# A fifth Strassen pair in the gates of two branches, and every second low part of the projections added up by transfers

## The chip, the cores and the metric

The kernel runs on one core of a Trainium2 chip. The metric is the device time of one execution in microseconds. TensorE (PE) multiplies, VectorE (DVE) and ScalarE (ACT) work element by element, GpSimd (POOL) does a little of that here and issues some transfers, and SyncE's queue (SP) issues the loads of the weights. Each engine works through its own instructions in order and waits for others by semaphores.

## The reference

One layer of a decoder trunk: one input projection feeds three mixers, each mixer's output is projected to the model width, the three results are merged by sigmoid gates computed from the input, and an output projection, a residual and a layer norm follow. All is float32, with 256 rows of 2048 channels.

```
u = x @ w_in[l]
(a_q, a_f, a_i, a_g, b_q, b_k, b_v, b_g,
 c_b, c_c, c_x, c_g, m_a, m_b, m_c) = jnp.split(u, split_idx, axis=-1)
o_a = hgrn2_mixer(a_q, a_f, a_i, lower_bounds[l])
o_a = o_a * lax.rsqrt(jnp.mean(jnp.square(o_a), axis=-1, keepdims=True) + RMS_EPS)
o_a = o_a.reshape(bsz, t, HGRN_WIDTH) * hgrn_norm_g[l].astype(jnp.float32)
y_a = (o_a.astype(x.dtype) * jax.nn.silu(a_g)) @ w_proj_hgrn[l]
o_b = swa_sink_attention(b_q, b_k, b_v, bias, attn_sinks[l])
y_b = (o_b * jax.nn.silu(b_g)) @ w_proj_attn[l]
o_c = short_gated_conv(c_b, c_c, c_x, conv_w[l])
y_c = (o_c * jax.nn.silu(c_g)) @ w_proj_conv[l]
merged = jax.nn.sigmoid(m_a) * y_a + jax.nn.sigmoid(m_b) * y_b + jax.nn.sigmoid(m_c) * y_c
y = merged @ w_out[l]
x = layer_norm(ALPHA * x + y, ln_g[l], ln_b[l])
```

## The kernel before

Every product of float32 operands is made of three matmuls. An operand is split into a high part `hi` (ScalarE casts it to fp32r, L114) and a low part `lo` (VectorE subtracts the high part from the raw value, L115), and TensorE adds hi x hi, hi x lo and lo x hi. x and the mixers' outputs are split once and stay in SBUF. The weights stream through: SP loads 1 MB granules `raw` (three buffers), each in two halves of 1024 columns (in the projections two k-tiles of 512), and each half is split into `hi` and `lo` (four buffers each) and used 12 times by TensorE. A program's scheduler sets the order of the instructions of each engine ahead of time.

The program has three parts. Up to about 525 us it does the input projections and the mixers; a list of generators, `tasks`, is advanced one step by `pump` behind every half granule, so that the mixers' work lies between the matmuls. From about 526 to 900 us it does the three branches, each in two halves: the gate's weights (`pair_of_groups`, 16 k-tiles as eight pairs p = 0..7, two output groups of 512 columns at once), and then two projections (`gemm`, four granules for each half in all), whose results are multiplied with the gates and added into `merged`. Then come the output projection (its first two groups by `pair_of_groups` too), residual and layer norm.

In `pair_of_groups` the pairs 1, 3, 5 and 7 go by Strassen's scheme (Winograd's form): the 2 x 2 blocks (two k-tiles by two column groups) of weights are added and subtracted into four sums, in a tile `w` of their own (L702 to L704), these are split into `hw` (ScalarE) and `lw` (VectorE), and seven products of blocks do instead of eight. A product is three matmuls of 512 columns (L677 to L679). The matching sums of x are made once, by `sums_of_x`, ahead of the branches, and those of the merged rows by `turn`. Eight partial sums p1 to p8 stay in PSUM until the last pair; then `one` is a copy of p1 and eight additions on VectorE (L727 to L734) give the two groups.

Of the kernel before, what the change touches and what calls it, by code (L numbers as in the profile page):

```python
# [44 lines left out]
PAIRS = (0, 1, 0, 1, 0, 1, 0, 1)  # L45
# [5 lines left out]
def hybrid_kernel(ctx, tc, a, out):  # L51
# [6 lines left out]
    lop = ctx.enter_context(tc.tile_pool(name="lop", bufs=4))  # L58
# [96 lines left out]
    def gemm(src, xs, n, major, first=None):  # L155
# [6 lines left out]
        for g in range(src.shape[0]):  # L162
# [4 lines left out]
            for s in range(2):  # L167
                hi, lo = halves[s] if first else split_w(raw[:, s])
# [31 lines left out]
    def constants():  # L200
# [15 lines left out]
        c["gn"] = const.tile([P, HW], F32, name="gn")  # L216
        nc.sync.dma_start(out=c["gn"], in_=a["hgrn_norm_g"].partition_broadcast(P))
# [335 lines left out]
    def sums_of_x():  # L553

        n = len(pairs)
        xr = rawp.tile([P, n, 2, T], F32, tag="raw", name="xr")
        for i, p in enumerate(pairs):
            nc.sync.dma_start(out=xr[:, i], in_=a["xT"][:, 2 * p : 2 * p + 2])
# [3 lines left out]
        for i in range(0, n, 2):  # L562
            dst = t8([P, 2, 4, 2, P], "sums", F32R)
            sums.append(dst)
            for j in range(2):
                split_to(dst[:, j], sx[:, :, i + j])
            yield
# [81 lines left out]
    msums = []  # L649

    def turn(m, d):
        dst = t8([P, 4, 2, T], "m", F32R)
        ms.append(dst)
        if d % 2 == 0:
            msums.append(t8([P, 2, 4, 2, P], "msums", F32R))
        for i, ps in transpose_pairs([[m[:, t, c * P : c * P + P] for t in range(2)] for c in range(4)], "mT"):
            split_to(dst[:, i : i + 2], ps)
            if PAIRS[2 * d + i // 2]:
# [269 lines left out]
```

## Time and profile before

| | |
|---|---|
| time, median of 3 runs (lowest to highest) | 1004.88 us (1003.66 to 1004.89) |
| the profiled execution: its time, its span | 1005.54 us, 1003.6 us |
| TensorE busy | 985.9 us, 98% of the span |
| VectorE, ScalarE, POOL busy | 808.5, 562.7, 33.0 us |
| mean granted clock of TensorE | 0.994 |
| data moved by transfers | 193.67 MB |

The time is taken from outside the span; the profile's rows are times within the span. An engine's busy time says what it did; where it waited, and for whom, is read from the idle time ahead of an instruction and from the time lines.

### The profile page before, as it was taken

The numbers are of one execution on the slowest core, as the hardware profiler recorded it, in microseconds if no ns is written. First come the engines' busy times: TensorE is split into PE (matmuls) and PEld (weight loads), VectorE is DVE, ScalarE is ACT, GpSimd is POOL, SyncE is SP. The second block draws the span as 40 slices with busy tenths as digits, with TensorE's granted clock in tenths as the row PEclk, the third lists the DMA queues.
The fourth block names the chain that finished last, engine by engine and source line by source line (L and its number), as shares of the span: only waits on it lengthen the run. The fifth ranks groups of instructions, "written<-read, shape, count | busy, mean of one in ns | idle before, by whom it ended". The sixth has DMA issues, their size and how long they took to land.

```text
span 1003.6 us, 13714 instructions
## 1 busy us (share of the span) xinstructions
PE 985.9 (98%) x5418; PEld 833.0 (83%) x5418; DVE 808.5 (81%) x1022; ACT 562.7 (56%) x735; POOL 33.0 (3%) x32
## 2 busy tenths in 40 slices
PE   8999999999999999999999999999999999999995
PEld 5888888888888888888888888888888888888884
DVE  6557889689965667768778898897989889897997
ACT  5545668557564655645655555555555555564551
POOL 1000100220010000000000000000000000000003
PEclk9999999999999999999999999999999999999998
DMA  8745545444455446544455655555556556548542
GB/s 315 262 172 206 173 163 171 166 171 169 169 182 196 174 162 196 182 169 166 174 200 178 220 198 206 210 205 194 216 183 210 209 195 215 180 169 336 205 167 84
DMA packets 30831, 193.67 MB, mean 193 GB/s; under 512 B 3840, under 2 KB 4640, under 8 KB 8752
## 3 DMA queue, kind: packets, MB, share of 16 engines
q1 hardware_dynamic: 28944, 185.90, 52.2%
q10 hardware_dynamic: 1152, 4.72, 1.2%
q0 software_dynamic: 672, 2.20, 0.8%
q8 instruction: 42, 0.69, 0.3%
q14 instruction: 21, 0.17, 0.0%
HBM read 190.68 MB, written 2.12 MB: 192 GB/s over the span
## 4 chain that ended last, share of the span: by engine, by line
PE 92%; DVE 5%; DMA 1%; issue 1%; ACT 1%; SPq 0%; DVEq 0%; ACTq 0%
PE acc L151 24%; PE acc L150 11%; PE acc L143 9%; PE p L677 9%; PE acc L145 9%; PE p L679 9%; PE p L678 9%; PE acc L144 9%; DVE lo L115 1%; PE acc L153 1%; PE sc L464 1%; PE pvb L507 1%; DMA raw<-in_w_rows 1%; DVE xres L799 1%; PE pT L497 1%
## 5 line engine op out<-in xcount | busy, mean ns | idle before, releaser
L114 ACT CAST hi<-raw 128x1024 fp32r<-128x1024 f32 (+1 forms) x341 | 343.9, 1013 | 320.6 <-PE p L678 107.3
L115 DVE TENSOR_TENSOR lo<-raw,hi 128x1024 fp32r<-128x1024 f32 (+1 forms) x341 | 396.9, 1175 | 107.3 <-ACT hi L114 105.5
L151 PE MATMUL acc<-xs,hi 128*128 128x512 f32 x1056 | 371.4, 396 | 0.0
L150 PE MATMUL acc<-xs,lo 128*128 128x256 f32 x990 | 278.4, 281 | 0.0
L151 PEld LDWEIGHTS acc<-xs,hi 128*128 128x128 f32 x1056 | 196.8, 188 | 43.4
L150 PEld LDWEIGHTS acc<-xs,lo 128*128 128x128 f32 x990 | 186.8, 189 | 2.4
L677 PE MATMUL p<-hi,xs 128*128 128x512 f32 x240 | 93.4, 389 | 0.0
L678 PE MATMUL p<-hi,xs 128*128 128x512 f32 x240 | 93.4, 389 | 0.0
L679 PE MATMUL p<-lo,xs 128*128 128x512 f32 x240 | 93.4, 389 | 0.0
L115 DVE TENSOR_TENSOR lw<-w,hw 128x2048 fp32r<-128x2048 f32 x28 | 64.2, 2292 | 22.2 <-ACT hw L114 20.8
L143 PE MATMUL acc<-hi,xs 128*128 128x512 f32 (+1 forms) x160 | 60.6, 379 | 2.3 <-ACT hi L114 2.3
L114 ACT CAST hw<-w 128x2048 fp32r<-128x2048 f32 x28 | 53.6, 1913 | 11.4 <-DVE w L704 11.2
L145 PE MATMUL acc<-lo,xs 128*128 128x512 f32 (+1 forms) x160 | 59.5, 374 | 0.0
L144 PE MATMUL acc<-hi,xs 128*128 128x512 f32 (+1 forms) x160 | 59.4, 371 | 0.0
L679 PEld LDWEIGHTS p<-lo,xs 128*128 128x128 f32 x240 | 45.1, 188 | 9.4
L678 PEld LDWEIGHTS p<-hi,xs 128*128 128x128 f32 x240 | 45.1, 188 | 9.3
L677 PEld LDWEIGHTS p<-hi,xs 128*128 128x128 f32 x240 | 45.0, 188 | 9.3
L191 ACT COPY rest<-acc 128x256 f32<-128x256 f32 x66 | 24.0, 372 | 42.3 <-PE acc L151 41.6
L143 PEld LDWEIGHTS acc<-hi,xs 128*128 128x128 f32 x160 | 30.4, 190 | 10.0 <-ACT hi L114 4.5
L145 PEld LDWEIGHTS acc<-lo,xs 128*128 128x128 f32 x160 | 30.4, 191 | 5.9 <-DVE lo L115 0.8
L702 DVE TENSOR_TENSOR w<-raw 128x1024 f32<-128x1024 f32 x28 | 34.2, 1221 | 1.2 <-DMA raw<-in_w_gate 0.9
L144 PEld LDWEIGHTS acc<-hi,xs 128*128 128x128 f32 x160 | 30.6, 191 | 4.9
(263 smaller groups left out, 1476.4 us busy)
## 6 DMA issues: line engine op xcount, KB each, us to landing
raw<-in_w_cols SPq DMA_DIRECT2D x68, 1024.0 KB, 4.8
raw<-in_w_gate SPq DMA_DIRECT2D x48, 1024.0 KB, 4.8
raw<-in_w_out SPq DMA_DIRECT2D x16, 1024.0 KB, 4.8
raw<-in_w_rows SPq DMA_DIRECT2D x12, 1024.0 KB, 4.8
raw<-in_w_proj_hgrn SPq DMA_DIRECT2D x8, 1024.0 KB, 4.7
raw<-in_w_proj_attn SPq DMA_DIRECT2D x8, 1024.0 KB, 4.8
raw<-in_w_proj_conv SPq DMA_DIRECT2D x8, 1024.0 KB, 4.8
raw<-in_w_rows SPq DMA_DIRECT2D x7, 512.0 KB, 9.2
```

The source lines that it names most:

```text
L114: nc.scalar.copy(out=hi, in_=r)
L115: nc.vector.tensor_sub(out=lo, in0=r, in1=f32(hi))
L143: nc.tensor.matmul(out=acc, lhsT=xk[:, 0, ts], rhs=hi, start=first, stop=False)
L144: nc.tensor.matmul(out=acc, lhsT=xk[:, 1, ts], rhs=hi, start=False, stop=False)
L145: nc.tensor.matmul(out=acc, lhsT=xk[:, 0, ts], rhs=lo, start=False, stop=last)
L150: nc.tensor.matmul(out=acc[:, :T], lhsT=lo, rhs=xk[:, 0], start=False, stop=False)
L151: nc.tensor.matmul(out=acc, lhsT=hi, rhs=xk, start=first, stop=last)
L191: nc.scalar.copy(out=rest[p], in_=acc[p, T:])
L677: nc.tensor.matmul(out=ps, lhsT=x[0], rhs=hi, start=begins, stop=False)
L678: nc.tensor.matmul(out=ps, lhsT=x[1], rhs=hi, start=False, stop=False)
L679: nc.tensor.matmul(out=ps, lhsT=x[0], rhs=lo, start=False, stop=last)
L702: nc.vector.tensor_sub(out=w[:, 0:2], in0=raw[:, 0:1].to_broadcast([P, 2, NC]), in1=raw[:, 1::2])
```

## The change

The Strassen pairs are now a list given to each call: (0, 2, 3, 5, 7) for the gates of the second and third branch, (0, 2, 5, 7) for the first branch and for the output projection. The sums of a Strassen pair are written over the raw block itself, by four subtractions of 512 columns, behind the splitting of the blocks that are needed as they are. In the projections the second half of every granule gets its low part in another way (`split_by_dma`): ScalarE writes the negated weights rounded into `lo`, a transfer on POOL's queue adds the raw weights to it, and ScalarE casts `hi` as before; `lo` has five buffers. The sums of x are made in three pieces of two, two and one pairs. The norm's weights of the first mixer are applied where its output is transposed and split, one scale to each row of channels, instead of by two multiplications on POOL.

```diff
-PAIRS = (0, 1, 0, 1, 0, 1, 0, 1)
+PAIRS, FEWER = (0, 2, 3, 5, 7), (0, 2, 5, 7)
...
-    lop = ctx.enter_context(tc.tile_pool(name="lop", bufs=4))
+    lop = ctx.enter_context(tc.tile_pool(name="lop", bufs=5))
...
+    def split_by_dma(r):
+        hi = hip.tile([P, HALF], F32R, tag="hi", name="hi")
+        lo = lop.tile([P, HALF], F32R, tag="lo", name="lo")
+        nc.scalar.mul(out=lo, in_=r, mul=-1.0)
+        nc.gpsimd.dma_start(out=lo, in_=r, accum_op=ALU.add)
+        nc.scalar.copy(out=hi, in_=r)
+        return hi, lo
...
-                hi, lo = halves[s] if first else split_w(raw[:, s])
+                hi, lo = halves[s] if first else split[s](raw[:, s])
...
-            split_to(outs["a"][hf][:, i : i + 2], ps)
+            for j in range(2):
+                g = C["gn"][:, 4 * hf + i + j : 4 * hf + i + j + 1]
+                dst = outs["a"][hf][:, i + j]
+                nc.scalar.mul(out=dst[:, 0], in_=ps[:, j], mul=g)
+                nc.vector.scalar_tensor_tensor(out=dst[:, 1], in0=ps[:, j], scalar=g, in1=f32(dst[:, 0]),
+                                               op0=ALU.mult, op1=ALU.subtract)
...
-        sx = t8([P, 4, n, P], "sx")
-        block_sums([sx[:, j] for j in range(4)], xr[:, :, 0, :P], xr[:, :, 1, :P], xr[:, :, 0, P:], xr[:, :, 1, P:])
-        yield
+        for at in range(0, len(PAIRS), 2):
+            n = len(PAIRS[at : at + 2])
+            xr = rawp.tile([P, n, 2, T], F32, tag="raw", name="xr")
...
-        nc.gpsimd.tensor_mul(out=gate, in0=gate,
-                             in1=C["gn"][:, hf * NC : hf * NC + NC].rearrange("p (o n) -> p o n", o=1)
-                             .to_broadcast([P, 2, NC]))
...
-            if not PAIRS[p]:
+            if p not in taken:
...
-            w = t8([P, 4, NC], "w")
-            nc.vector.tensor_sub(out=w[:, 0:2], in0=raw[:, 0:1].to_broadcast([P, 2, NC]), in1=raw[:, 1::2])
-            nc.vector.tensor_sub(out=w[:, 2], in0=raw[:, 3], in1=w[:, 0])
-            nc.vector.tensor_sub(out=w[:, 3], in0=raw[:, 2], in1=w[:, 2])
             hi, lo = split_w(flat[:, NC : 3 * NC])
...
+            nc.vector.tensor_sub(out=raw[:, 1], in0=raw[:, 0], in1=raw[:, 1])
+            nc.vector.tensor_sub(out=raw[:, 0], in0=raw[:, 0], in1=raw[:, 3])
+            nc.vector.tensor_sub(out=raw[:, 3], in0=raw[:, 3], in1=raw[:, 1])
+            nc.vector.tensor_sub(out=raw[:, 2], in0=raw[:, 2], in1=raw[:, 3])
...
-            split_w(w, hw, lw)
+            split_w(raw, hw, lw)
...
-            for n, y in enumerate(whole + summed + rest if raw_first or end else summed + rest[::-1] + whole):
+            for n, y in enumerate(whole + summed + rest if p else rest + summed[::-1] + whole):
...
-            sg = pair_of_groups(a["w_gate"][2 * n + half], xs, sums, n > 0, 2 if n else 1)
+            sg = pair_of_groups(a["w_gate"][2 * n + half], xs, sums, PAIRS if n else FEWER, 2 if n else 1)
...
-                acc = gemm(a[wp][d], outs[br], NC, "rows")
+                acc = gemm(a[wp][d], outs[br], NC, "rows", split=(split_w, split_by_dma))
...
-    y = pair_of_groups(a["w_out2"][0], ms, msums, False, 0)
+    y = pair_of_groups(a["w_out2"][0], ms, msums, FEWER, 0)
```

The scheduler writes the order of the instructions anew. TensorE has 4769 rows in it now and had 4781. Three places follow, in the order of the rows of one engine.

VectorE in the first gate half of the second branch, from pair 3 to pair 5, before (`raw_6135` is the weights of pair 3, `raw_6101` of pair 2, `raw_6208` of pair 5; `w` is the tile of the sums):

```order
L702 TENSOR_TENSOR w_6137<-raw_6135 128x1024
L115 TENSOR_TENSOR lo_6104<-raw_6101,hi_6103 128x1024
L703 TENSOR_TENSOR w_6137<-raw_6135,w_6137 128x512
L704 TENSOR_TENSOR w_6137<-raw_6135,w_6137 128x512
L115 TENSOR_TENSOR lo_6120<-raw_6101,hi_6119 128x1024
L115 TENSOR_TENSOR lw_6150<-w_6137,hw_6149 128x2048
L115 TENSOR_TENSOR lo_6142<-raw_6135,hi_6141 128x1024
L115 TENSOR_TENSOR lo_6146<-raw_6135,hi_6145 128x512
L702 TENSOR_TENSOR w_6210<-raw_6208 128x1024
L703 TENSOR_TENSOR w_6210<-raw_6208,w_6210 128x512
```

The same stretch of the new program, from pair 2 to pair 4 (`raw_6131` is pair 2, `raw_6170` pair 3, `raw_6209` pair 4):

```order
L721 TENSOR_TENSOR raw_6131<-raw_6131 128x512
L722 TENSOR_TENSOR raw_6131<-raw_6131 128x512
L115 TENSOR_TENSOR lo_6173<-raw_6170,hi_6172 128x1024
L719 TENSOR_TENSOR raw_6170<-raw_6170 128x512
L115 TENSOR_TENSOR lw_6146<-raw_6131,hw_6145 128x2048
L115 TENSOR_TENSOR lo_6177<-raw_6170,hi_6176 128x512
L720 TENSOR_TENSOR raw_6170<-raw_6170 128x512
L115 TENSOR_TENSOR lo_6212<-raw_6209,hi_6211 128x1024
L721 TENSOR_TENSOR raw_6170<-raw_6170 128x512
L115 TENSOR_TENSOR lo_6228<-raw_6209,hi_6227 128x1024
L115 TENSOR_TENSOR lw_6185<-raw_6170,hw_6184 128x2048
```

Before, a pair's sums stood ahead of the low parts of its blocks and needed only `raw`; the pair's two low parts came after `lw`. Now the subtractions stand behind the pair's own low parts, and those of pair 3 are spread between low parts of pair 4.

ScalarE at the end of a gate half of the second branch, before (`hw_6295` belongs to pair 7, `raw_6337` and `raw_6371` are the first two granules of the projection; `one` is the copy of p1):

```order
L114 CAST hw_6295<-w_6283 128x2048
L114 CAST hi_6287<-raw_6281 128x1024
L114 CAST hi_6291<-raw_6281 128x512
L114 CAST hi_6339<-raw_6337 128x1024
L114 CAST hi_6355<-raw_6337 128x1024
L726 COPY one_6323<-p1_6020 128x512
L114 CAST hi_6373<-raw_6371 128x1024
L114 CAST hi_6389<-raw_6371 128x1024
```

And now (`hw_6330` belongs to pair 7, `raw_6372` and `raw_6407` are the projection's first two granules; `lo_6391` is the negated copy to which the transfer adds):

```order
L114 CAST hw_6257<-raw_6243 128x2048
L114 CAST hi_6374<-raw_6372 128x1024
L114 CAST hw_6330<-raw_6316 128x2048
L740 COPY one_6358<-p1_6050 128x512
L122 ACTIVATE lo_6391<-raw_6372 128x1024
L124 CAST hi_6390<-raw_6372 128x1024
L114 CAST hi_6409<-raw_6407 128x1024
L124 CAST hi_6425<-raw_6407 128x1024
L122 ACTIVATE lo_6426<-raw_6407 128x1024
```

Before, the casts of the second half of the first granule stood ahead of the copy of p1; now the negation that the first transfer needs stands behind hw and that copy.

VectorE near the end of the second mixer, before (`sx` is the block sums of x, `den` and `s` belong to attention, whose transposes `pT` on TensorE read `s`):

```order
L115 TENSOR_TENSOR lo_4742<-raw_4719,hi_4741 128x1024
L545 TENSOR_TENSOR yc_1839<-yc_4379,hc_4271 128x512
L549 TENSOR_TENSOR sx_4806<-sx_4806,xr_4801 128x512
L550 TENSOR_TENSOR sx_4806<-xr_4801 128x512
L551 TENSOR_TENSOR sx_4806<-xr_4801,sx_4806 128x512
L486 TENSOR_TENSOR den_4623<-den_4623,es_4621 128x4
L487 RECIPROCAL den_4623<-den_4623 128x4
L488 TENSOR_TENSOR s_4607<-s_4607,den_4623 128x1024
L115 TENSOR_TENSOR lo_4782<-raw_4779,hi_4781 128x1024
```

The same place now:

```order
L500 TENSOR_TENSOR den_4629<-den_4629,es_4627 128x4
L501 RECIPROCAL den_4629<-den_4629 128x4
L502 TENSOR_TENSOR s_4613<-s_4613,den_4629 128x1024
L115 TENSOR_TENSOR lo_4788<-raw_4785,hi_4787 128x1024
L115 TENSOR_TENSOR lo_4816<-raw_4785,hi_4815 128x1024
L514 TENSOR_TENSOR pT_4710<-pT_4711,pT_4709 128x512
L514 TENSOR_TENSOR pT_4710<-pT_4718,pT_4709 128x512
L562 TENSOR_TENSOR sx_4810<-xr_4807 128x256
L564 TENSOR_TENSOR sx_4810<-xr_4807 128x256
L563 TENSOR_TENSOR sx_4810<-sx_4810,xr_4807 128x256
L115 TENSOR_TENSOR lo_4843<-raw_4840,hi_4842 128x1024
L565 TENSOR_TENSOR sx_4810<-xr_4807,sx_4810 128x256
```

The four block sums stood around and ahead of `s` and now stand behind it, in pieces of 256 columns.

## Rows read from the trace of the kernel before

**Rows 1.** The page's busy line, and the chain that ended last.

```profile
PE 985.9 (98%) x5418; PEld 833.0 (83%) x5418; DVE 808.5 (81%) x1022; ACT 562.7 (56%) x735; POOL 33.0 (3%) x32
...
PE 92%; DVE 5%; DMA 1%; issue 1%; ACT 1%; SPq 0%; DVEq 0%; ACTq 0%
```

**Rows 2.** Windows, third branch: us, then each engine's busy time, PEclk, DMA share, GB/s.

```profile
776.20:817.00 40.80, 40.80 (x182) 33.78 (x181) 35.52 (x37) 21.90 (x21) 0.00 (x0) 1.00 0.56 201
817.00:839.00 22.00, 22.00 (x99) 18.22 (x98) 18.85 (x22) 11.54 (x12) 0.00 (x0) 1.00 0.59 207
```

**Rows 3.** Time line of TensorE at a gate's start: start us, us, instruction.

```profile
776.15 0.39 PE L677 MATMUL p<-hi,xs 128*128 128x512 f32 x1
...
776.60 0.39 PE L679 MATMUL p<-lo,xs 128*128 128x512 f32 x1
```

**Rows 4.** Groups of VectorE by kind, 526 to 925 us: busy us, mean ns | idle.

```profile
L115 DVE TENSOR_TENSOR lo<-raw,hi 128x1024 fp32r<-128x1024 f32 x126 | 153.2, 1221 | 28.6 <-ACT hi L114 28.0
L115 DVE TENSOR_TENSOR lw<-w,hw 128x2048 fp32r<-128x2048 f32 x24 | 55.0, 2292 | 19.5 <-ACT hw L114 18.1 <-PE p L679 1.4
L702 DVE TENSOR_TENSOR w<-raw 128x1024 f32<-128x1024 f32 x24 | 29.3, 1221 | 1.2 <-DMA raw<-in_w_gate 0.9 <-DMA raw<-in_w_out 0.2
...
L703 DVE TENSOR_TENSOR w<-raw,w 128x512 f32<-128x512 f32 x23 | 15.8, 688 | 0.3
```

**Rows 5.** Groups of ScalarE by kind, the same stretch.

```profile
L114 ACT CAST hi<-raw 128x1024 fp32r<-128x1024 f32 x128 | 134.5, 1053 | 145.6 <-PE p L678 87.5 <-PE acc L144 38.7 <-issue 12.5
L114 ACT CAST hw<-w 128x2048 fp32r<-128x2048 f32 x24 | 45.9, 1912 | 4.6 <-DVE w L704 4.4
...
L726 ACT COPY one<-p 128x512 f32<-128x512 f32 x6 | 3.5, 580 | 0.0
```

**Rows 6.** Time line of VectorE, third branch, first half.

```profile
783.83 0.69 DVE L703 TENSOR_TENSOR w<-raw,w 128x512 f32<-128x512 f32 x1
784.43 1.22 DVE L115 TENSOR_TENSOR lo<-raw,hi 128x1024 fp32r<-128x1024 f32 x1
785.57 0.69 DVE L704 TENSOR_TENSOR w<-raw,w 128x512 f32<-128x512 f32 x1
...
788.23 2.29 DVE L115 TENSOR_TENSOR lw<-w,hw 128x2048 fp32r<-128x2048 f32 x1 [1.24 <-ACT hw L114]
790.44 1.22 DVE L115 TENSOR_TENSOR lo<-raw,hi 128x1024 fp32r<-128x1024 f32 x1
```

**Rows 7.** Time line of TensorE, the first use of that lw.

```profile
793.60 0.39 PE L679 MATMUL p<-lw,sums 128*128 128x512 f32 x1
```

**Rows 8.** Transfers: queue, KB each, median us from issue to landing.

```profile
raw<-in_w_gate SPq DMA_DIRECT2D x48, 1024.0 KB, 4.8
...
xr<-in_xT SPq DMA_DIRECT2D x11, 256.0 KB, 7.8
bias<-bias_dr POOLq DMA_DIRECT2D x2, 1024.0 KB, 6.5
...
neg<-in_negmask POOLq DMA_DIRECT2D x1, 24.0 KB, 4.1
...
rb<-in_rel_bias POOLq DMA_DIRECT2D x1, 2.0 KB, 3.5
```

**Rows 9.** POOL's groups, the costliest line.

```profile
L596 POOL TENSOR_TENSOR ga<-ga,gn 128x1024 f32<-128x1024 f32 x2 | 6.6, 3317 | 100.5 <-DVE ga L197 100.5
```

**Rows 10.** Time lines of VectorE, then of TensorE, near 484 us.

```profile
477.95 0.69 DVE L548 TENSOR_TENSOR sx<-xr 128x512 f32<-128x512 f32 x1 [1.39 <-DMA xr<-in_xT]
...
484.44 1.22 DVE L488 TENSOR_TENSOR s<-s,den 128x1024 f32<-128x1024 f32 x1
...
484.17 0.39 PE L151 MATMUL acc<-xs,hi 128*128 128x512 f32 x1
485.81 0.95 PE L497 MATMUL pT<-ident,s 128*128 128x128 f32 x7 [1.26 <-DVE s L488]
```

**Rows 11.** Time line of TensorE in the last output product.

```profile
943.59 0.50 PE L679 MATMUL p<-lw,msums 128*128 128x512 f32 x1 [0.37 <-DVE lw L115]
```

More of the change, by code (lines that the diff above doesn't have):

```diff
@@ L153, in columns, with gemm @@
             nc.tensor.matmul(out=acc[:, :T], lhsT=lo, rhs=xk[:, 0], start=False, stop=False)
-    def gemm(src, xs, n, major, first=None):
+    def gemm(src, xs, n, major, first=None, split=(split_w, split_w)):
         acc = accumulators()
@@ L215, in constants @@
         nc.vector.tensor_copy(out=c["mask"], in_=mask)
-        c["gn"] = const.tile([P, HW], F32, name="gn")
-        nc.sync.dma_start(out=c["gn"], in_=a["hgrn_norm_g"].partition_broadcast(P))
+        c["gn"] = const.tile([P, 8], F32, name="gn")
+        nc.sync.dma_start(out=c["gn"], in_=a["hgrn_norm_g"])
         c["cw"] = const.tile([P, 8, 3], F32, name="cw")
@@ L553, in sums_of_x @@
     def sums_of_x():
[L555 to L558, printed above, removed]
-        sx = t8([P, 4, n, P], "sx")
-        block_sums([sx[:, j] for j in range(4)], xr[:, :, 0, :P], xr[:, :, 1, :P], xr[:, :, 0, P:], xr[:, :, 1, P:])
-        yield
[L562 to L566, printed above, removed]
+        for at in range(0, len(PAIRS), 2):
+            n = len(PAIRS[at : at + 2])
+            xr = rawp.tile([P, n, 2, T], F32, tag="raw", name="xr")
+            for i, p in enumerate(PAIRS[at : at + 2]):
+                nc.sync.dma_start(out=xr[:, i], in_=a["xT"][:, 2 * p : 2 * p + 2])
+            sx = t4([P, 4, n, P], "sx")
+            block_sums([sx[:, j] for j in range(4)], xr[:, :, 0, :P], xr[:, :, 1, :P], xr[:, :, 0, P:], xr[:, :, 1, P:])
+            yield
+            dst = t8([P, n, 4, 2, P], "sums", F32R)
+            for i, p in enumerate(PAIRS[at : at + 2]):
+                sums[p] = dst[:, i]
+                split_to(dst[:, i], sx[:, :, i])
             yield
@@ L636, in hybrid_kernel @@
         tasks.append(attn(hf, q, kz, vb, gate))
-    pairs = [p for p in range(KT // 2) if PAIRS[p]]
-    sums = []
+    sums = {}
     tasks.append(sums_of_x())
@@ L647, in hybrid_kernel @@
     ms = []
-    msums = []
+    msums, dsts = {}, []
     def turn(m, d):
@@ L662, in turn, with pair_of_groups @@
                 block_sums([sx[:, j] for j in range(4)], raw[:, 0, :P], raw[:, 1, :P], raw[:, 0, P:], raw[:, 1, P:])
-                split_to(msums[d // 2][:, d % 2], sx)
+                split_to(msums[p], sx)
             yield
-    def pair_of_groups(src, x, sums, raw_first, spare):
+    def pair_of_groups(src, x, sums, taken, spare):
         p1, p2, p6, p7 = [accp.tile([P, NC], F32, tag="acc", name=f"p{i}") for i in (1, 2, 6, 7)]
@@ L684, in pair_of_groups @@
         last = KT // 2 - 1
-        final = max(p for p in range(KT // 2) if not PAIRS[p])
+        final = max(p for p in range(KT // 2) if p not in taken)
         for p in range(KT // 2):
@@ L708, in pair_of_groups @@
             split_w(flat[:, 3 * NC :], hi2, lo2)
-            i = pairs.index(p)
-            hw, lw = [t8([P, 4, NC], name, F32R) if i % 2 and n < spare else
+            nc.vector.tensor_sub(out=raw[:, 1], in0=raw[:, 0], in1=raw[:, 1])
+            nc.vector.tensor_sub(out=raw[:, 0], in0=raw[:, 0], in1=raw[:, 3])
+            nc.vector.tensor_sub(out=raw[:, 3], in0=raw[:, 3], in1=raw[:, 1])
+            nc.vector.tensor_sub(out=raw[:, 2], in0=raw[:, 2], in1=raw[:, 3])
+            i = taken.index(p)
+            hw, lw = [t8([P, 4, NC], name, F32R) if i % 2 and n >= 2 - spare else
                       mgp.tile([P, 4, NC], F32R, tag=name, name=name) for n, name in enumerate(("hw", "lw"))]
-            split_w(w, hw, lw)
-            sx = [[sums[i // 2][:, i % 2, j, m] for m in range(2)] for j in range(4)]
+            split_w(raw, hw, lw)
+            sx = [[sums[p][:, j, m] for m in range(2)] for j in range(4)]
             k = 2 * p
```

15 lines of the change are left out of this document (9 added, 6 removed).

## The prediction

> **What bounds the kernel now.** I began with the page's busy line and its chain of work that ended last [rows 1]: TensorE is busy 98% of the span and owns 92% of the chain; VectorE owns 5%, DMA 1%. So a microsecond comes off only if matmuls go, or one of TensorE's few waits goes, and everything else may grow only as long as it stays hidden. The table by stretches [rows 2] asks how much it may grow in the third branch: in a gate's pair stage (776.2 to 817) VectorE works 35.5 of 40.8 us, in the two projections behind it 18.9 of 22.0. TensorE does not wait at all there, and its granted clock is 1.00, the upper level. Then the time line for what one matmul costs: two with 512 columns start 0.23 us apart [rows 3] (776.15 to 776.60 is two of them, so 0.226 each, although each shows 0.39 of duration). The views of VectorE and ScalarE by kind of instruction [rows 4, 5] give what preparing weights costs, and VectorE's time line [rows 6] how densely such instructions follow one another: 0.60 us for 512 columns, 1.14 for 1024, 2.21 for 2048. Last, the slack: the low part of the sums that starts at 788.23 ends at 790.52, and TensorE first asks for it at 793.60 [rows 7], 3.08 us later.
>
> **What goes: 12 matmuls.** A plain pair is 8 products, 24 matmuls; a Strassen pair 7 products, 21. Branches two and three have four gate halves, and each gets one more Strassen pair; branch one and the last output product keep four. So 4 x 3 = 12 matmuls go: 12 x 0.226 = **-2.7 us**, and that is all that TensorE itself gives.
>
> **A wait ahead of the branches.** At 484.17 TensorE stops until 485.81 for a transpose that needs VectorE's s [rows 10]. VectorE was late: at 477.95 it had stood 1.39 us for the block xr of x, and before s, which it began at 484.44, it had the other three block sums of 0.60 us to do. In the new order all of the block sums stand behind this s (front, third place in the order). Without the 1.39 and the four sums (2.4) s comes 3.8 us earlier, more than the 1.64 between those two starts. One matmul's 0.23 is not a wait, so I book **-1.4 us**; the bounds are -1.4 and 0, since three smaller loads of x now take raw buffers one after the other between the weights of the columns, and one of them could be waited for instead.
>
> **VectorE's work moves, it doesn't shrink.** Before, a Strassen pair costs it lo 1.14, lo of the fourth block 0.60, w 1.14, two subtractions 1.20 and lw 2.21, in all 6.3; a plain pair 2 x 1.14 = 2.3. Four of each: 34.3 us, against the 35.5 measured, so about 1.2 of other work (the tail of the half before) lies in the stage. After, the subtractions are four of 0.60 instead of 1.14 + 1.20: a Strassen pair is 6.35; five, and three plain ones: 31.8 + 6.8 = 38.6, with the 1.2 39.8. TensorE's stage shrinks from 40.8 to 40.1. VectorE goes from 87% to 99% of it. In the projections eight low parts become four: 18.9 - 4 x 1.14 = 14.3 of 22. It can't work ahead from there: hi has four buffers, raw three, and a raw buffer is now held until lw is done, where before the sums had a tile of their own. I went through the first half of the second branch by hand, instruction by instruction, in the new order: each starts when its engine, its inputs and its buffer are free, with the durations of [rows 4 to 6] and 4.8 for a load [rows 8]. Set TensorE's first gate matmul at 0. The low parts of the sums come at 3.1, 13.3, 22.2, 33.5 and 40.3 and are asked for at 3.2, 13.4, 22.2, 33.3 and 39.9. A slack of 3 us becomes none, and what is late is the last: 0.4 us. **Four halves: +1.6 us.** The bounds are 0 (VectorE 1% faster than so worked out) and 2 us a half (0.05 more for each of its 40-odd instructions).
>
> **The sum by transfer.** ScalarE writes the negated weights (1.05, as its cast [rows 5]), POOL's queue adds the raw ones into them. POOL had 6.6 us of multiplications with the norm's weights, which go, and is otherwise idle [rows 9]; ScalarE works 21.9 and 11.5 us of the two stages [rows 2] and gets four negations in the second, 4.2. Neither is a bound. The landing is. ScalarE's order (front, second place) puts the first negated part of a half behind the last hw, which itself stands behind the last pair's four subtractions: hw is ready at 37.9, the copy of p1 takes 0.58, the negation 1.05: 39.5. TensorE asks for this lo 191 matmuls after the start, 191 x 0.226 = 43.3, with the 0.4 above 43.7 or 43.8. **The window is 4.3 us.** The second and third windows are 7.5 and 8.5, the branch-one halves have 5.7 and more. How long does a 512 KB accumulating transfer take? No row shows one. From below: transfers on POOL's queue of 2 and 24 KB land after 3.5 and 4.1 us; from above: the 1 MB one after 6.5 [rows 8]. A straight line from 24 KB to 1 MB gives 4.1 + 0.49 x 2.4 = 5.3; the sum is read and written in SBUF, but it has a second operand to read, so I take 5.4. Late by 1.1, four halves (branches two and three): **+4.4 us**. Bounds: 3.5, hidden; 6.5, +8.8; and 8, with weight loads in flight 0.56 of the time [rows 2], +14.8.
>
> For the price there is a page. The Trainium skill, "DMA: Bandwidth & Descriptors", section "Anatomy of one DMA", gives 2.0 us plus bytes/436,000 for this path, an estimate of 3.2 us for 512 KB; by it nothing is late and the sum is 4.4 lower. The trace does not agree where it can be asked: the same formula gives 4.4 for 1 MB, and the row has 6.5 [rows 8]; 2.1 more would be 5.3 here.
>
> **Hidden or small.** The norm's scale becomes small ScalarE and VectorE operations at the transposed output: four of each a half, and both engines have spare time there by the page (VectorE 81%, ScalarE 56% over the span [rows 1]). The last output product has waits of about a microsecond now (one is 0.37 idle before lw's matmul at 943.59 [rows 11]); its first Strassen pair comes earlier and its sums are in place: 0, with 1 us to either side.
>
> **The sum.** 1005.54 (the profiled run) - 2.7 - 1.4 + 1.6 + 4.4 = 1007.4. That run stands 0.66 over the median of the runs shown, 1004.88, against which I forecast: **1006.8 us**.
>
> **Rivals.** *All hidden, faster.* The transfer lands within 4.3 us and VectorE keeps up: 1004.88 - 2.7 - 1.4 = 1000.8, to 1002.4 with the 0.4 a half. For it: small transfers on this queue take 3.5 and 4.1, and in SBUF no memory outside is read. Against it: the 6.5 of the 1 MB one. It decides at 4.3 us. The skill's formula above is this case.
> *The transfer is late by 2 us or more.* It shares the 16 DMA engines with 1 MB weight loads; a 256 KB load of x took 7.8 us among others, more than a 1 MB one's 4.8 alone [rows 8]. At 6.5 the time is 1004.88 - 2.5 + 8.8 = 1011.2; at 7.8, 1016.4. The skill, same page, section "Issuing engines are not separate DMA queues", says the same of the engines; the row of 7.8 agrees.
> *VectorE becomes the bound.* At 99% a little more per instruction, or a scheduler's order that lets lw wait for hw, costs directly: 2 us a half instead of 0.4 gives 1004.88 - 4.1 + 8 + 4.4 = 1013.2. For it: each lw waits for a hw that waits for subtractions, and VectorE waits with it unless the order offers other work.
> *Nothing measurable*, because the first two windows' lateness is about a microsecond: 1002.9 to 1006.9, inside the forecast's own range.
>
> **How the numbers follow.** Forecast case (the transfer lands in 4.3 to 6 us, half a microsecond a half): 1002.4 to 1009, chance 0.40. All hidden 0.33, late transfer 0.17, VectorE bound 0.10. About 0.2%, 2 us, is what a measurement of this kernel can tell. Faster (below 1002.9): 0.31 of "all hidden" and 0.05 of the forecast, 0.36. Same: 0.02 + 0.21 = 0.23. Slower: 0.14 + 0.17 + 0.10 = 0.41. Signs are mixed because a gain of 4.1 stands against one price that no row shows. The range: from 1000 (all hidden, and some of the last product's waits gone) to 1014 (the transfer at about 7.3, or VectorE at 2 us a half), leaving out about 0.15.
>
> **What would show it.** 12 matmuls fewer; no wait at the transpose near 484; in the second and third branch's pair stages VectorE near 39 of 40 us and TensorE waits below half a microsecond before the last lw; each of those four halves with one wait of about 1.1 us at the first projection's second half, released by a DMA on POOL's queue that took about 5.4 us. Wrong if that transfer takes below 4.3 or above 6.5 us, if waits appear at other projections' granules or at raw buffers that a transfer still holds, or if the gate stages show waits at every lw.

## The result, and the profile after

The changed kernel takes 1057.92 us (median of 4 runs, 1054.34 to 3496.65) against 1004.88 us (4 runs, 1003.66 to 1005.81): ratio 1.0517, 95% interval 1.0475 to 1.0559. It is 5% slower, outside the range. One of its four executions took 3496.65 us and is left out of the ratio; the median of the other three is 1055.46 us, and no run of the experiments showed the like.

The page of the changed kernel, as in [rows 1] and [rows 8] of the kernel before: the busy line, the chain that ended last, and two kinds of transfers with their median time from issue to landing.

```profile
PE 1005.4 (95%) x5406; PEld 835.1 (79%) x5406; DVE 804.9 (76%) x1059; ACT 588.7 (56%) x768; POOL 46.6 (4%) x54
...
PE 79%; DMA 10%; DVE 5%; issue 3%; ACT 2%; SPq 0%; POOLq 0%; ACTq 0%
...
lo<-raw POOLq DMA_DIRECT2D x24, 512.0 KB, 6.5
raw<-in_w_proj_hgrn SPq DMA_DIRECT2D x8, 1024.0 KB, 7.6
```

The same loads of the first branch in the kernel before:

```profile
raw<-in_w_proj_hgrn SPq DMA_DIRECT2D x8, 1024.0 KB, 4.7
```

TensorE's share of the chain fell from 92% to 79%, and DMA's rose from 1% to 10%. The new transfers landed after 6.5 us (4.4 to 10.5), and weight loads of the first branch after 7.6 instead of 4.7.

Where the 50.1 us between the spans (1003.6 and 1053.7) lie, by the time lines of TensorE. A projection is counted from its first matmul behind the last one of its gate: in four halves of the changed kernel 3 to 8 of the projection's matmuls stand among the gate's last and count, with the waits between them, as the gate's.

| stage | before | after | difference |
|---|---|---|---|
| up to the first gate | 525.8 | 525.0 | -0.7 |
| six gates of the branches | 245.0 | 259.1 | +14.1 |
| six pairs of projections | 133.5 | 165.0 | +31.5 |
| output product, first part | 22.8 | 22.8 | 0 |
| output product by Strassen | 41.5 | 43.6 | +2.1 |
| last columns, layer norm | 35.2 | 38.2 | +3.0 |

So most of the loss is in the projections, 4.6 to 6.1 us in each of the six halves. The stretches of the third branch answer to [rows 2]: the first is its first gate half without the last 4 us, the second these 4 us and the projection behind them; the third line is 3 us inside that projection.

```profile
808.00:847.00 39.00, 38.53 (x166) 30.34 (x165) 36.11 (x39) 20.52 (x19) 0.00 (x0) 1.00 0.51 189
847.00:877.00 30.00, 26.21 (x107) 21.16 (x108) 19.16 (x24) 17.66 (x19) 3.45 (x4) 0.94 0.77 219
857.70:860.90 3.20, 3.20 (x9) 2.52 (x8) 1.23 (x1) 3.20 (x4) 0.00 (x0) 0.51 1.03 352
```

The DMA share around a projection went from 0.59 to between 0.77 and 0.92 (the latter in the first branch), VectorE is busy 19.2 of these 30 us where it was busy 18.9 of 22, and right after a wait the granted clock stands at 0.51, the lower of its two levels. Time lines of four engines show one such place (start, duration, instruction, idle time and what ended it), and the start of the first branch ahead of it:

```profile
528.02 0.49 PE L692 MATMUL p<-lo,xs 128*128 128x512 f32 x1 [0.64 <-DVE lo L115]
529.39 0.53 PE L690 MATMUL p<-hw,xs 128*128 128x512 f32 x1 [0.88 <-ACT hw L114]
...
849.16 0.86 POOL L123 DMA_DIRECT2D lo<-raw  x1 [49.75 <-ACT lo L122]
849.78 7.56 SPq L108 DMA_DIRECT2D raw<-in_w_proj_conv  x2
852.96 0.86 POOL L123 DMA_DIRECT2D lo<-raw  x1 [2.94 <-ACT lo L122]
853.30 0.39 PE L153 MATMUL acc<-hi,oc 128*128 128x512 f32 x1
857.00 0.50 PE L154 MATMUL acc<-lo,oc 128*128 128x512 f32 x1 [3.31 <-DMA lo<-raw]
857.34 0.56 PE L152 MATMUL acc<-hi,oc 128*128 128x512 f32 x1
858.12 0.63 PE L154 MATMUL acc<-lo,oc 128*128 128x512 f32 x1
857.22 1.05 ACT L114 CAST hi<-raw 128x1024 fp32r<-128x1024 f32 x1 [4.56 <-DMA raw<-in_w_proj_conv]
861.42 0.86 POOL L123 DMA_DIRECT2D lo<-raw  x1 [7.60 <-ACT lo L122]
```

At the start of the first branch (528.02, 529.39) TensorE waits for pair 0's low part and hw, as it did not before. In the third branch the first transfer of this half is issued at 849.16, 0.6 us ahead of a weight load (the SPq row holds two issues, at 849.78 and 857.01). By their landings the transfer takes 7.80 us and that load 7.35. TensorE would come to the low part at about 853.5, one matmul behind 853.30, and gets it at 857.00; its matmuls then start up to 0.43 us apart instead of 0.23. ScalarE meanwhile waits 4.56 us for the load, and so the next negation and the third transfer (861.42) are late too. Taken over the branches and the output product, starts of 512-column matmuls more than 0.45 us apart hold 35.3 us of waiting in 27 places (before: 0.5 us in one), and some 14 us more lie in about 95 matmuls at 0.29 to 0.45 apart (before: 1 us).

The waits by queue and engine from 526 to 960 us, TensorE's to 1020 (us in total, times, longest):

```profile
SPq L701 <- DVE lw L115: 113.7, 16, 11.7
SPq L701 <- DMA lo<-raw: 85.8, 15, 8.6
SPq L108 <- DVE lw L115: 83.4, 12, 10.8
SPq L108 <- DMA lo<-raw: 54.0, 9, 9.5
...
ACT hi L114 <- DMA raw<-in_w_gate: 36.6, 18, 3.6
ACT hi L114 <- DMA raw<-in_w_proj_attn: 13.4, 2, 7.6
ACT hi L114 <- DMA raw<-in_w_proj_hgrn: 10.8, 3, 5.4
...
PE acc L154 <- DMA lo<-raw: 23.5, 11, 4.5
PE p L690 <- ACT hw L114: 4.7, 7, 1.4
```

The load queue and ScalarE's one wait for a load in the kernel before, from 526 to 960 us:

```profile
SPq L688 <- DVE lo L115: 252.2, 51, 11.5
SPq L108 <- DVE lo L115: 144.3, 30, 9.0
...
ACT hi L114 <- DMA raw<-in_w_out: 3.3, 1, 3.3
```

There the load queue waits 81 times for a plain low part and never for lw, and ScalarE waits 3.3 us for one load. Now a load is issued when lw is done (28 times) or when a transfer has landed (24 times), and ScalarE waits 70 us for loads.

### The profile page after: what moved, and what is told of

The parts are those of the page before. It is cut to its first block, busy times and chain, and to the rows that moved or that the text cites. A ratio compares the mean times of both kernels' runs of the same rounds, so it can differ in the third digit from the quotient of the medians.

```text
span 1053.7 us, 13776 instructions
## 1 busy us (share of the span) xinstructions
PE 1005.4 (95%) x5406; PEld 835.1 (79%) x5406; DVE 804.9 (76%) x1059; ACT 588.7 (56%) x768; POOL 46.6 (4%) x54
## 4 chain that ended last, share of the span: by engine, by line
PE 79%; DMA 10%; DVE 5%; issue 3%; ACT 2%; SPq 0%; POOLq 0%; ACTq 0%
PE acc L160 23%; PE acc L159 11%; PE p L692 8%; PE p L690 7%; PE p L691 7%; PE acc L154 6%; PE acc L152 6%; PE acc L153 5%; DMA lo<-raw 5%; DMA raw<-in_w_proj_hgrn 2%; DVE lw L115 2%; DMA raw<-in_w_gate 1%; ACT hi L114 1%; ACT hw L114 1%; DMA raw<-in_w_proj_attn 1%
## 5 line engine op out<-in xcount | busy, mean ns | idle before, releaser
L114 ACT CAST hi<-raw 128x1024 fp32r<-128x1024 f32 (+1 forms) x317 | 315.9, 1005 | 331.6 <-PE p L691 86.9
L115 DVE TENSOR_TENSOR lo<-raw,hi 128x1024 fp32r<-128x1024 f32 (+1 forms) x317 | 365.8, 1164 | 142.9 <-ACT hi L114 141.4
L690 PE MATMUL p<-hi,xs 128*128 128x512 f32 x216 | 84.4, 391 | 0.1
L692 PE MATMUL p<-lo,xs 128*128 128x512 f32 x216 | 83.7, 390 | 0.6 <-DVE lo L115 0.6
L691 PE MATMUL p<-hi,xs 128*128 128x512 f32 x216 | 84.1, 390 | 0.0
L115 DVE TENSOR_TENSOR lw<-raw,hw 128x2048 fp32r<-128x2048 f32 x32 | 73.3, 2291 | 12.8 <-ACT hw L114 12.8
L114 ACT CAST hw<-raw 128x2048 fp32r<-128x2048 f32 x32 | 61.1, 1908 | 12.2 <-DVE raw L722 12.2
L690 PEld LDWEIGHTS p<-hi,xs 128*128 128x128 f32 x216 | 40.7, 188 | 9.1 <-ACT hi L114 0.5
L691 PEld LDWEIGHTS p<-hi,xs 128*128 128x128 f32 x216 | 40.7, 188 | 8.7
L123 POOL DMA_DIRECT2D lo<-raw x24 | 20.8, 867 | 527.6 <-ACT lo L122 512.4
L152 PEld LDWEIGHTS acc<-hi,xs 128*128 128x128 f32 x160 | 30.5, 190 | 9.8 <-ACT hi L114 4.1
L154 PE MATMUL acc<-lo,ob 128*128 128x512 f32 x64 | 26.9, 420 | 9.2 <-DMA lo<-raw 8.8
L690 PE MATMUL p<-hw,sums 128*128 128x512 f32 x84 | 34.3, 408 | 1.3 <-ACT hw L114 1.3
```

Source lines behind the costliest of these rows:

```text
L114: nc.scalar.copy(out=hi, in_=r)
L115: nc.vector.tensor_sub(out=lo, in0=r, in1=f32(hi))
L123: nc.gpsimd.dma_start(out=lo, in_=r, accum_op=ALU.add)
L152: nc.tensor.matmul(out=acc, lhsT=xk[:, 0, ts], rhs=hi, start=first, stop=False)
L154: nc.tensor.matmul(out=acc, lhsT=xk[:, 0, ts], rhs=lo, start=False, stop=last)
L690: nc.tensor.matmul(out=ps, lhsT=x[0], rhs=hi, start=begins, stop=False)
```

## The experiments

Theory A at the start: transfers and weight loads slow each other. Theory B: the fifth pair and the sums in place make VectorE the bound. Times are medians; each ratio is against the kernel before on the same chip.

| run | time, us | ratio (95% interval) |
|---|---|---|
| e1_no_transfer | 1015.12 | 1.0106 (1.0090 to 1.0121) |
| e2_transfer_only | 1009.85 | 1.0053 (1.0038 to 1.0068) |
| e3_four_pairs | 1052.79 | 1.0476 (1.0457 to 1.0496) |
| e4_four_no_transfer | 1016.22 | 1.0121 (1.0106 to 1.0136) |
| e5_own_tile | 1014.36 | 1.0092 (1.0074 to 1.0110) |
| e6_own_tile_no_transfer | 1014.27 | 1.0093 (1.0077 to 1.0109) |
| e7_fourth_raw | 1048.83 | 1.0440 (1.0423 to 1.0456) |
| e8_odd_pairs | 1016.14 | 1.0109 (1.0088 to 1.0131) |
| e9_norm_and_pieces | 1005.42 | 1.0003 (0.9994 to 1.0012) |
| e10_five_own_tile | 1008.35 | 1.0033 (1.0021 to 1.0046) |
| e11_idle_transfers | 1057.16 | 1.0518 (1.0499 to 1.0538) |
| e12_five_own_transfer | 1032.09 | 1.0279 (1.0257 to 1.0301) |
| e13_idle_two_tiles | 1031.48 | 1.0266 (1.0237 to 1.0294) |
| e14_small_hold | 1016.84 | 1.0119 (1.0103 to 1.0136) |
| e15_full_hold | 1036.47 | 1.0310 (1.0285 to 1.0334) |
| e16_best | 1002.55 | 0.9974 (0.9965 to 0.9984) |

**e1, e2, e3, e4: the parts apart.** From the changed kernel (e1, e3, e4) and from the kernel before (e2, with the changed `split_by_dma`, norm scale and five low-part buffers):

```diff
# e1, e4
-acc = gemm(a[wp][d], outs[br], NC, "rows", split=(split_w, split_by_dma))
+acc = gemm(a[wp][d], outs[br], NC, "rows")
# e3, e4
-sg = pair_of_groups(..., sums, PAIRS if n else FEWER, 2 if n else 1)
+sg = pair_of_groups(..., sums, FEWER, 2 if n else 1)
# e2
-acc = gemm(a[wp][d], outs[br], NC, "rows")
+acc = gemm(a[wp][d], outs[br], NC, "rows", split=(split_w, split_by_dma))
```

> All of the change but the transfers: every low part of the projections is subtracted on VectorE again. Theory A (accumulating transfers and weight loads slow each other, which makes the low parts late and the raw buffers late after them, and TensorE's clock falls behind each long wait): all 31.5 us lost in the projections come back and most of the 14.1 lost in the gates; time 1002 to 1008. Theory B (the fifth pair and the sums in place make VectorE the bound; the gates' losses are its own): the gates keep 42 to 45 us each, time 1012 to 1022.

> The kernel before with only the transfers, five low-part buffers and the norm's scale at the output (which frees the space for the fifth buffer); four Strassen pairs with sums in a tile of their own. Theory A: each of the six projection stages takes 25 to 28 us instead of 21.76, the gates behind them start late by late weights, time 1030 to 1052. Theory B: the transfers hide behind the slack of 3 us that the four pairs leave, or cost only the first window of a half; time under 1015.

> The changed kernel with four Strassen pairs (0, 2, 5, 7) in every gate, transfers kept. Theory A: nearly as slow as the changed kernel, 1045 to 1060 (12 matmuls more, 2.7 us, a little less pressure on VectorE). Theory B: the gates of branches two and three go back to about 40.8 us each, time 1035 to 1045.

> The changed kernel with four Strassen pairs everywhere and no transfers: what stays is the sums in place, the order of the pairs, the norm's scale and the block sums in pieces. Both theories: about as before, 1002 to 1006; below 1004 if the wait of 1.4 us near 484 is gone and nothing else is new. If it is over 1008, the sums in place (raw held until lw is done) cost by themselves, and theory A's part shrinks by as much.

Neither theory holds, though each has times in its range (B those of e1 and e2, A that of e3). The transfers alone cost 5.3 us on the kernel before (A wanted 25 to 47). The fifth pair costs nothing (1015.1 with it, 1016.2 without; B wanted more with it). What is left of the change without transfers and without the fifth pair costs 11.6, where I expected none. And the two together cost far more than their sum: with the sums in place, transfers add 40.3 (1055.5 over 1015.1) or 36.6 (1052.8 over 1016.2). Transfers and loads in e2, with the waits of its load queue and of TensorE for transfers, then in e3:

```profile
raw<-in_w_gate SPq DMA_DIRECT2D x48, 1024.0 KB, 4.8
lo<-raw POOLq DMA_DIRECT2D x24, 512.0 KB, 5.7
raw<-in_w_proj_hgrn SPq DMA_DIRECT2D x8, 1024.0 KB, 5.0
...
SPq L108 <- DMA lo<-raw: 65.2, 9, 9.5
SPq L699 <- DMA lo<-raw: 64.3, 15, 9.6
...
PE acc L154 <- DMA lo<-raw: 2.1, 4, 0.9
```

```profile
raw<-in_w_gate SPq DMA_DIRECT2D x48, 1024.0 KB, 6.1
lo<-raw POOLq DMA_DIRECT2D x24, 512.0 KB, 8.3
raw<-in_w_proj_hgrn SPq DMA_DIRECT2D x8, 1024.0 KB, 7.7
```

The same transfers take 5.7 beside loads of 4.8 to 5.0, or 8.3 beside loads of 6.1 to 7.7. In e2, too, 24 loads were issued only when a transfer had landed, and every transfer lay beside a load for a while: by issues and landings for 3.4 us in the median, in the changed kernel for 6.1. So neither is the loss by itself. And in e4, with no transfers at all, what did SP and ScalarE wait for?

```profile
SPq L701 <- DVE lw L115: 110.0, 14, 11.5
SPq L108 <- DVE lw L115: 101.8, 12, 10.6
...
ACT hi L114 <- DMA raw<-in_w_gate: 21.0, 6, 4.7
```

26 loads wait for lw, since the sums stand in the weight buffer. Each load comes that much later, and ScalarE already waits 21 us for loads.

**e5 to e8: is it the buffer?** Theory C: a raw buffer held until lw is done takes the loads' lead away, so that loads and transfers meet. Theory D: the order, pair 0 first and sums behind the low parts. In e5 and e6 the sums go to a tile of their own, which also puts them ahead of the low parts again, with pairs 0, 2, 5, 7 (e6 without transfers); e7 is e3's form with a fourth buffer for every fourth load; e8 has the sums in place, no transfers, and pairs 1, 3, 5, 7.

```diff
# e5, e6
+w = t8([P, 4, NC], "w")
+nc.vector.tensor_sub(out=w[:, 0:2], in0=raw[:, 0:1].to_broadcast([P, 2, NC]), in1=raw[:, 1::2])
...
-split_w(raw, hw, lw)
+split_w(w, hw, lw)
# e7
+if len(late) % 4 == 1:
+    return t8(shape, "raw")
# e8
-PAIRS, FEWER = (0, 2, 3, 5, 7), (0, 2, 5, 7)
+PAIRS, FEWER = (1, 3, 5, 7), (1, 3, 5, 7)
```

> As the run with four pairs and transfers (1052.8), but the four sums are written to a tile of their own, as in the kernel before, so that a raw buffer is free as soon as its low parts and subtractions are done. Neither theory A nor B explains 1009.9 with transfers alone beside 1052.8 in this form. Theory C (raw held until lw is done takes the lead of the weight loads away; then loads and transfers meet, each slows the other, and the next load waits for the transfer): 1008 to 1016, loads about 5 us ahead of the transfers again. Theory D (it is the order, pair 0 first and the low parts behind the sums, that makes everything late): 1040 to 1055.

> The same without transfers; beside the run with four pairs in place and no transfers (1016.2) it tells what the sums in place cost alone. Theory C: 1004 to 1010, the rest of the difference to before being the wait at the first branch's start, where pair 0 now needs its sums first. Theory D: 1013 to 1018, nothing comes back.

> As the run with four pairs and transfers (1052.8), sums in place, but every fourth load of weights behind the mixers goes to a fourth buffer, taken from the pool that the sums' tile had. Theory C: the lead comes back by another way, 1008 to 1025. Theory D, or a contention that needs no lack of buffers: 1040 to 1055.

> Sums in place, no transfers, but the pairs are 1, 3, 5 and 7 everywhere, as before. Theory C: the 4.4 us lost at the first branch's start go, the half microsecond to two lost in each gate by lw just in time stays: 1008 to 1013. Theory D: 1003 to 1006.

e5 is as C wanted: 38 us come back by one tile. That its 1014.36 equals e6's 1014.27 doesn't make the transfers free: e6 has a stall of 4.9 us in the output product that e5's profile does not show (that profile is of an execution of 1022.83 us, 8.5 above the median, so its rows are not used further). e6 is 4 above C's range and inside D's: the gates from the second on are all back at 40.8 to 40.9 us, but the first takes 44.7 (pair 0's sums at the very start), and there is the stall. e7's 1048.8 lies in D's range: its first five projection stages shrink to 21.8 to 24.5 us, from e3's 26.1 to 30.0, but the last takes 42.7, where SP waited up to 22 us for a transfer to release a buffer ahead of it in its queue. So the fourth buffer's sign is right in five stages of six, and its time decides nothing. e8 lies above both ranges: the first gate takes 42.3 instead of e4's 45.4, but gates of 42.9 in the last three halves, and an end that is 1.7 longer than e4's and 4.5 longer than before, eat that: the order of the pairs moves the loss about. Since the tile of e5 also changes the place of the sums, e5 does not by itself tell the held buffer from that order; for the buffer speak e7's five stages, with the sums still in place, and e4's waits for lw. How much is the order's is not shown.

**e9, e10, e12: what can be kept.** e9 is the kernel before with the norm's scale and the block sums in pieces. e10 has five pairs (0, 2, 3, 5, 7) in branches two and three, 2, 3, 5, 7 in the first and 1, 3, 5, 7 at the end, sums in a tile of their own, no transfers; e12 is e10 with transfers. Both have four low-part buffers, since the fifth pair's sums of x need the space of the fifth.

```diff
# e10 against e6
-PAIRS, FEWER = (0, 2, 5, 7), (0, 2, 5, 7)
+PAIRS, FIRST, FEWER = (0, 2, 3, 5, 7), (2, 3, 5, 7), (1, 3, 5, 7)
...
-    lop = ctx.enter_context(tc.tile_pool(name="lop", bufs=5))
+    lop = ctx.enter_context(tc.tile_pool(name="lop", bufs=4))
...
+dst = t8(...) if n == 2 else const.tile([P, n, 4, 2, P], F32R, name="sums5")
```

> The kernel before with only the norm's scale at the output and the block sums of x in pieces. The prediction's second term alone: the wait at the transpose near 484 shrinks from 1.65 us to about 0.5, as in the changed kernel; time 1003.4 to 1004.2. If 1004.6 or more, the loads of x in pieces cost elsewhere what this gives.

> What the runs so far point to: the fifth pair kept, its sums in a tile of their own, no transfers, and no call that begins with a Strassen pair at a stage's start that has just waited: pairs 0, 2, 3, 5, 7 in branches two and three, 2, 3, 5, 7 in branch one, 1, 3, 5, 7 at the end, four low-part buffers. Theory C (the loss came from raw buffers held by lw and by transfers, and from pair 0 first): gates of branches two and three at 40.1 to 40.6 us, time 1001 to 1004. Theory B (VectorE is the bound at five pairs): gates at 41 to 43, time 1005 to 1012.

> As the five pairs with a tile of their own, with the transfers. Theory C: the loop doesn't close, since only the transfers hold raw buffers, not lw: 3 to 8 us above the same without transfers, as they cost 5.3 on the kernel before. If the loop closes in projections alone: 1030 or more.

e9 is unchanged (1.0003): the wait at the transpose is gone, and the Strassen stage of the output product takes 1.2 us more in its profile, which is of an execution 1.8 us above the median. e10's gates are close to theory C's (40.3 to 40.7); its time is in B's range, since the end takes 39.2 us instead of 35.2, behind a copy of p1 that ScalarE's order puts behind other casts. e12 falsifies my expectation of 3 to 8: 24 us, 10.9 of them TensorE's waits for transfers, with the loads at 4.8 to 4.9 in the median and the transfers at 6.0. So 24 us can be lost to transfers with the sums in a tile of their own and most loads not slowed. Whether the five pairs or the four low-part buffers did it the run does not separate, and the five pairs of e16 were not run with transfers.

**e11, e13, e14, e15: traffic, hold or wait?** On four pairs with sums in place, low parts on VectorE. The negation and a transfer go into spare tiles that nobody reads, so TensorE never waits for one, and the transfer reads the resident x (e11, e13: traffic alone), four columns of the weights (e14: hold alone) or all 1024 (e15: both).

```diff
-nc.scalar.mul(out=lo, in_=r, mul=-1.0)
-nc.gpsimd.dma_start(out=lo, in_=r, accum_op=ALU.add)
-nc.scalar.copy(out=hi, in_=r)
-return hi, lo
+nc.scalar.mul(out=spare, in_=r, mul=-1.0)
+nc.gpsimd.dma_start(out=spare, in_=x0, accum_op=ALU.add)                # e11 one spare, e13 two
+nc.gpsimd.dma_start(out=spare[:, :4], in_=r[:, :4], accum_op=ALU.add)   # e14 instead
+nc.gpsimd.dma_start(out=spare, in_=r, accum_op=ALU.add)                 # e15 instead
+return split_w(r)
```

> Four pairs with the sums in place (1016.2 without transfers, 1052.8 with them). Every second half granule of the projections starts the same negation and the same 512 KB accumulating transfer, but into a spare tile and from the resident x: nobody waits for it and it holds no weight buffer, the low part is subtracted on VectorE. Output as before. Theory C1 (contention alone: the transfers slow the loads): loads of 7 to 9 us, 1035 to 1050. Theory C2 (the transfer holds the raw buffer, so the next load starts at its landing and meets the next transfer, a loop): loads at most 6 to 7 us where they overlap, time 1016 to 1024.

> Four pairs, sums in place, low parts on VectorE; every second half granule of the projections also starts a 512 KB accumulating transfer from the resident x into one of two spare tiles in turn, so that ScalarE does not wait for an earlier transfer as it did for 43 us with one spare tile. No weight buffer is held. If contention for the DMA engines is enough: 1035 or more. If ScalarE's wait for the spare tile made the 41 us of the run before: 1016 to 1025.

> The same, but the transfer moves only four columns (2 KB) of the raw weights into the spare tile: it holds the weight buffer until it lands (3 to 4 us by the small ones on POOL's queue) and moves next to nothing. If holding the buffer closes the loop by itself: 1025 to 1045. If it takes the traffic: 1016 to 1022.

> The same with the whole 512 KB from the raw weights into the spare tile: hold and traffic together, but TensorE never waits for the transfer, since the low part comes from VectorE. If hold and traffic make the loop: 1035 to 1055, with ScalarE waiting for loads as in the changed kernel. If the loss is the wait for the low part itself: 1016 to 1024.

e11 tells little: ScalarE waited 43 us for its one spare tile. e13, without that (7.5 us left), lies between its two expectations: traffic alone costs 15.3 us (1031.5 over e4's 1016.2), or 14.6 over e14, which makes the same negations. A hold of 2.9 us costs nothing (e14, 1016.8); one as long as the full transfer's was not run without its traffic. Both cost 20.3 (e15), and the two intervals touch (1.0237 to 1.0294, 1.0285 to 1.0334). The 16 us that remain up to e3's 36.6 appear where TensorE needs the result; that is the difference of two runs, whose engine orders differ too. Transfers of e13, then of e14:

```profile
raw<-in_w_gate SPq DMA_DIRECT2D x48, 1024.0 KB, 6.6
spare<-xs POOLq DMA_DIRECT2D x24, 512.0 KB, 8.3
```

```profile
raw<-in_w_gate SPq DMA_DIRECT2D x48, 1024.0 KB, 4.8
spare<-raw POOLq DMA_DIRECT2D x24, 2.0 KB, 2.9
```

Loads of 6.6 against 4.8 us: loads and transfers slow each other with nobody waiting for the transfer. In e15 TensorE's waits stand in the gates, not in the projections:

```profile
PE p L693 <- ACT hw L114: 9.1, 6, 2.9
PE p L695 <- DVE lo L115: 4.1, 4, 2.5
...
ACT hi L114 <- DMA raw<-in_w_gate: 45.0, 14, 5.4
```

**e16: a version that beats both.** Five pairs (1, 3, 4, 5, 7) in branches two and three, everything else in the order of the kernel before, sums in a tile of their own, no transfers.

```diff
# against e10
-PAIRS, FIRST, FEWER = (0, 2, 3, 5, 7), (2, 3, 5, 7), (1, 3, 5, 7)
+PAIRS, FIRST, FEWER = (1, 3, 4, 5, 7), (1, 3, 5, 7), (1, 3, 5, 7)
...
-for n, y in enumerate(whole + summed + rest if p else rest + summed[::-1] + whole):
+for n, y in enumerate(whole + summed + rest if raw_first or end else summed + rest[::-1] + whole):
```

> A fifth pair (1, 3, 4, 5, 7) in branches two and three only, all else in the order of before, sums in a tile of their own, no transfers, norm's scale and block sums as changed. Theory: the branches' gates at 40.1 to 40.7, the end as before; 1001 to 1004.5. The gain of 12 matmuls is 2.7 at most; the run with 0, 2, 3, 5, 7 kept 0.1 to 0.5 a half.

1002.55 us, ratio 0.9974 (0.9965 to 0.9984): faster than both, by 0.26% against the kernel before. Three of its four gates with five pairs, in windows:

```profile
650.84:691.29 40.45, 40.45 (x178) 33.08 (x177) 36.47 (x36) 22.75 (x22) 0.00 (x0) 1.00 0.53 191
775.59:815.77 40.18, 40.18 (x179) 33.15 (x177) 37.87 (x38) 23.05 (x23) 0.00 (x0) 1.00 0.54 193
837.53:877.85 40.32, 40.32 (x178) 33.00 (x177) 38.12 (x38) 22.93 (x23) 0.00 (x0) 1.00 0.54 195
```

VectorE is busy 37.9 of 40.2 us with five pairs, and TensorE does not wait in any gate: VectorE can carry five pairs when the sums have a tile of their own, as in e10. The fourth such gate has 12 of the projection's matmuls among its last; with its projections it takes 62.5 us where it took 62.6 before, and the other three halves are 0.4 to 0.6 us shorter.

## Why the prediction was wrong

**The step that failed** is "The sum by transfer": "Late by 1.1, four halves: +4.4 us". It took a landing time of 5.4 us as a property of the transfer, and "4.8 for a load" as one of the load. Two transfers late in the changed kernel, with little or nothing beside them, took 4.4 us; the median was 6.5 and the longest 10.5, and loads beside a transfer took 6.5 us in the median, the others 4.8. e2, with early loads, cost 5.3 us, close to the 4.4 forecast, but partly by luck: TensorE's own waits for transfers are 2.1 us there, in four places, and not four times 1.1. In the changed kernel a transfer lay beside loads for nearly twice as long (6.1 us against 3.4). The windows of 4.3, 7.5 and 8.5 us were worked out with loads that arrive early, and these windows shrink with the loads: TensorE waited 23.5 us for transfers in 11 places, and the six projection stages took 31.5 us more. "The branch-one halves have 5.7 and more" was wrong in the same way: they lost 10.7 us in their projections.

**"A slack of 3 us becomes none" was right and its consequence missed.** I took the vanished slack as a price of 0.4 us a half. The loads lost their lead with it: in e4 26 of them are issued at lw's end, and ScalarE waits 21.0 us for loads of the gates where before it waited for none of these. A kernel with little lead turns later delays into waits, and of those the transfers brought more.

**The rival "the transfer is late by 2 us or more"** had the mechanism (shared DMA engines) and the price per transfer, 6.5, which is what the median came to. It gave 1011, since it let only four transfers be late, each by itself. TensorE's direct waits for transfers are 23.5 us, about half of the loss. Beside those stand late loads, late sums, and matmuls at 0.43 us apart, none of which it counted.

**VectorE as the bound** was not it: in e1, without transfers, VectorE is busy 38.6 of the 42.4 us of a five-pair gate in the third branch, 91% and not 99, and e1 and e4 differ by 1.1 us the other way. The rival's price of 2 us a half was near all the same: e1's four halves cost some 1.5 each.

**12 matmuls, -2.7 us**: they went (5418 to 5406), and e16 shows what they are worth with early loads: 2.5 us by its median, with the norm's scale and the block sums in pieces, which alone gave nothing (e9); in its profile the four halves with five pairs are 1.5 us shorter in all, so the full 2.7 is not seen there. **The wait at 484**: it shrank as forecast, from 1.64 to 0.52 us between the starts; e9 shows nothing of it in the time.

**The sums in place, +1.6 us**: mis-sized. Without transfers the change costs 10.6 us (e1). By stages of its profile, some 6 beyond the 2.7 gained lie in the four halves with five pairs, 3.7 in the first branch, and 1.5 in the output product and the end. The first of these was priced at 0.4 a half, for low parts of the sums that come late; what TensorE waited for was mostly their high parts hw (in e1 2.2 us in four places, for lw 0.2 in one), which the prediction did not follow. The start of the first branch, where TensorE now waits for pair 0's low part and hw (and, in the changed kernel, the granted clock then falls to 0.50), was not priced at all. Which part of this is the order and which the held buffer stays open: e6 and e8 each undo a part, and neither returns to the time before; e16, which undoes both, is faster than it.

## What to carry to other kernels

Ask of a wait or a buffer that you remove who used the time of it as a lead: a buffer that is held longer can cost little alone and still make the transfers behind it late. A transfer that takes over an engine's work has to be priced beside the loads that are in flight then, in both directions, and on a kernel whose loads have lost their lead the two prices don't add. When two changes share buffers, run each alone and both together; here the transfers alone cost 5 us, the rest of the change 11, and both together 51.

## What the runs showed of the hardware

The 512 KB accumulating transfer within SBUF took 4.4 us with nothing or little beside it; the seven longest in the changed kernel took 8.0 to 10.5 us, beside 1 MB loads that took 6.5 to 9.5 us instead of 4.8 (e13 shows the same with a transfer that nobody needs, in medians: 8.3 and 6.6). By the packets on POOL's queue, 144 for each transfer, taken in their order, the two transfers of 4.4 us began to move 1.44 us after the issue and moved for 2.65; the three of over 10 us began after 4.5 to 4.8 and moved for 5.2 to 5.7. So both the start and the movement are slowed. Whether VectorE's work delays the start was not tested; one of the two that began after 1.44 us did so with VectorE busy all that time (942.3). The Trainium skill, "DMA: Bandwidth & Descriptors", section "Issuing engines are not separate DMA queues", says that transfers of all queues interleave on the same engines; these rows agree. The fit in the same page of the Trainium skill, section "Anatomy of one DMA", gives an estimate of 3.2 us for 512 KB; the shortest here, 4.4, is over it.

TensorE's granted clock fell to 0.50 to 0.54 for some 3 us after waits that put 3.7 to 4.9 us between two starts (up to 716.8, 857.0 and 925.4 us), and matmuls of 512 columns then started 0.43 us apart: a wait in the middle of dense work cost up to 1.7 us more than its own length. It fell too after starts 2.2 and 2.4 us apart (up to 658.4 and 792.2), and did not after 3.7 us up to 589.3, so the length of a wait alone did not tell its price.
